# A hand-written MLP order on one Trainium2 core: the passage from one unit to the next, rewritten

## The chip, the core and the metric

The kernel runs on one core of a Trainium2 chip. TensorE (PE in the profile) multiplies matrices into PSUM, which has eight banks of 128 partitions x 512 fp32 numbers. ScalarE (ACT) and VectorE (DVE) empty these banks and prepare operands in SBUF. SyncE (SP) issues the loads of weights, GpSimd (POOL) the DMAs that add results into the residual stream. Each engine works through its own instructions in the order in which the program has them, and waits on semaphores for what others must deliver. The metric is the device time of one execution in microseconds, the median of several.

## The reference, cut to what matters

A trunk of two layers over 256 tokens of width 2048, in fp32, with another attention in each layer. The change touches the MLP's order above all, and the projections' slightly:

```python
for i in range(DEPTH):                       # 2
    proj = _rmsnorm(x, g_attn[i]) @ w_in[i]  # 2048 x 5120
    ...
    x = x + merged @ w_out[i]                # 2048 x 2048
    hm = _rmsnorm(x, g_mlp[i])
    x = x + jnp.square(jax.nn.relu(hm @ w_mlp1[i])) @ w_mlp2[i]   # 2048 x 8192, 8192 x 2048
return _rmsnorm(x, g_final)
```

## The kernel before

**Products.** An fp32 operand is split into a rounded high part and the rest: ACT copies it to the high part (L117), DVE subtracts that from it (L118). A product is then three matmuls into the same bank, high by high, high by low and low by high (`passes`, L609 to L611).

**The MLP.** The 8192 hidden features are taken in eight units of 1024. Unit 0 is multiplied plainly (`up_plain`), in the part that a scheduler orders. Units 1 to 7 use a 2x2 block scheme with seven products, p1 to p7, in place of eight. A unit's products take eight steps over the 2048 inner features; a step adds 21 matmuls of 512 columns, three for each product, into seven banks. The eighth bank rotates: it takes the down product's groups (`psd`) and the turned blocks (`pu`).

**Factors.** The weights of a step are combined first (`up_weights`, `prep_up`). From two loaded tiles b and o DVE makes the sums s (L229) and o (L233, L235), and each of b, one half of o, s and the new o is split into a high and a low part: bh and bl, oh, sh and sl, th and tl. These are 6.95 us of DVE and some 3.4 us of ACT per step. p1 and p3 use b, p2 uses oh, p5 and p7 use s, p6 and p4 use t. Seven buffers hold one step's factors.

**The hand-written order** (`tc.manual_schedule()`, L736 to L763). While unit c+1 is multiplied up, unit c is multiplied down. Eight groups g make a unit: in group g the kernel issues one step of the next unit (`step_up`), the factors of the step after (`prep_up`), and 24 matmuls of the down product (`group_down`), whose bank ACT copies to `part` with a scale (L703) and POOL adds to x by DMA (L704). The down product's weights come in pieces of 256 rows, `raw_d`, split into `hi_d` and `lo_d` (`prep_down`); four buffers of each hold one bank's.

**The passage.** With g = 6 a unit's products end. `end_up` empties the seven banks with DVE additions (L659 to L668) into four blocks u0 to u3; ACT applies relu and square to each (L614, L615). With g = 7 the first step of the unit after follows into the banks as they come free. With g = 0 comes the second step, and between its products PE turns the four blocks: four transposes each into the rotating bank (`pu`, L681), which ACT and DVE split into `hT` (L117, L118). The next block, or the next `psd`, can start when DVE has read the bank. There are six passages in each layer, twelve in all; the start of the written order, with unit 0's blocks, and its end, with unit 7's, are like half a passage each. In names such as `pu_012` the digits are the layer, the unit and the block; `psd0031` is layer 0, unit 0, column block 3, token half 1.

Of the kernel before, what the change touches and what calls it, by code (L numbers as in the profile page):

```python
# [9 lines left out]
F32 = mybir.dt.float32  # L10
# [28 lines left out]
WH = 4  # L39
# [19 lines left out]
def trunk(ctx: ExitStack, tc: tile.TileContext, x, mem, g_attn, w_in, w_out, lambda_qk,  # L59
# [69 lines left out]
    def gemm_feat(w, acts, nm, raws=(None,) * 4):  # L129

        ps = [bank([P, 2, 256], f"ps_{nm}_{j}", True) for j in range(2)]
        for pc in range(4):
            wt = weights(w[pc * 512:(pc + 1) * 512, :], 4, 256, f"{nm}_{pc}", raws[pc])
            for kk in range(4):
                k = 4 * pc + kk
                hi, lo = wt[kk]
                a = acts[k // 4][:, k % 4]
                for j in range(2):
                    last = k == KT - 1
                    cols = slice(j * P, (j + 1) * P)  # L140

                    def low(**f):
                        nc.tensor.matmul(ps[j][:, 0, :], lo[:, cols], a[:, 0, :], **f)  # L143

                    def high(**f):
                        nc.tensor.matmul(ps[j].rearrange("p h t -> p (h t)"), hi[:, cols], a.rearrange("p h t -> p (h t)"), **f)  # L146

                    if last:
                        low(start=False, stop=False)
                        high(start=False, stop=True)  # L150
                    else:
                        high(start=(k == 0), stop=False)
                        low(start=False, stop=False)
# [56 lines left out]
    def up_weights(w, kp, f0, nm):  # L210
# [25 lines left out]
        t1, t3 = pieces(s, 2, "s")  # L236
        t2, t4 = pieces(o, 2, "t")
# [203 lines left out]
    for i in range(DEPTH):  # L441
# [175 lines left out]
        def up_plain():  # L617

            u = {}
            for f in range(2):  # L620
                ps = [bank([P, 512], f"pu0_{i}{f}{t}", True) for t in range(2)]
                for kp in range(KP):
                    wt = weights(w_mlp1[i][kp * 256:(kp + 1) * 256, f * 512:(f + 1) * 512], 2, 512, f"u0{i}{f}{kp}")
                    for a in range(2):
                        for t in range(2):
                            passes(ps[t], comb[kp][:, 2 * t + a], *wt[a], kp == a == 0, kp == KP - 1 and a == 1)
                for t in range(2):
# [6 lines left out]
        def prep_up(c, kp):  # L634

            making = up_weights(w_mlp1[i], kp, c * 1024, f"{i}{c}{kp}")
            for _ in range(2):
# [4 lines left out]
        def step_up(c, kp, turns=None, prep=None):  # L642
# [3 lines left out]
            for n, (hi, lo) in facts.pop((c, kp)).items():  # L646
                if turns and n in ("p1", "p3", "p5", "p6"):
                    next(turns)
                    if n in ("p1", "p5"):
                        next(prep)  # L650
                passes(banks[c][n], comb[kp][:, FACTORS.index(n)], hi, lo, kp == 0, kp == KP - 1)

        def end_up(c):

# [13 lines left out]
            nc.vector.tensor_tensor(c21, u3, ps["p4"], op=ALU.add)  # L668
            yield
            squared(m22, m22, -1.0)  # L670
            squared(c21, c21, 1.0)
            ublk[c] = ((c11, 0, 0), (m12, 0, 1), (c21, 1, 0), (m22, 1, 1))
# [12 lines left out]

        def prep_down(c, n, halves):

            for h in halves:
                for k in (4 * h, 4 * h + 2):
                    r0 = c * 1024 + k * P  # L690
# [144 lines left out]
```

## Time and profile before

| | us |
|---|---|
| time, median of 3 runs | 2298.21 |
| lowest and highest | 2297.55, 2300.5 |
| profiled execution | 2299.35 |
| its span, first to last instruction | 2297.6 |
| PE busy | 2207.4 |
| DVE busy | 1715.9 |
| ACT busy | 1332.0 |
| granted PE clock, mean share of full | 0.981 |

The span is what the trace covers; 1.75 us of the profiled execution lie around it. A busy engine isn't one at its peak: PE's matmuls are pipelined, so that each is listed with 0.39 us while the next starts 0.23 us later, and the durations of ACT and DVE overlap in the same way by some 0.1 us. What counts is the distance from one start to the next.

### The profile page before, as it was taken

The page shows a single profiled execution, that of the slowest core. Times are in us where ns is not written, and L with a number is a line of the kernel's source. Part 1 is how long each engine was busy: PE and PEld are TensorE (multiplying, and loading weights), DVE is VectorE, ACT ScalarE, POOL GpSimd, SP SyncE. Part 2 cuts the span into 40 slices and gives each one's busy share as a digit, 9 for nine tenths or more (in the row PEclk, how much of TensorE's full clock was granted, in tenths as well). Part 3 has the DMA queues.
Part 4 walks back from the last instruction along what each step waited for, and adds up shares of the span by engine and source line. Part 5 has one row for each costly group of instructions (what it writes and reads, how often), then busy time and mean ns, then how long its engine had stood idle before and what let it go on. Part 6 is the DMA issues. An engine that isn't in the chain of part 4 may idle for free.

```text
span 2297.6 us, 28469 instructions
## 1 busy us (share of the span) xinstructions
PE 2207.4 (96%) x10358; PEld 1814.3 (79%) x10358; DVE 1715.9 (75%) x2084; ACT 1332.0 (58%) x1840; POOL 115.4 (5%) x146
## 2 busy tenths in 40 slices
PE   9999999999999999999999999999999999999998
PEld 7888878887787787777878888887877778777786
DVE  6557766758888888888866665665888888888875
ACT  7445554655666666666655554465666666666664
POOL 0000000000000000000000000000000000000000
PEclk9999999999999999999999999999999999999999
DMA  7664555666676676676745556566767668667664
GB/s 242 193 192 151 169 163 187 184 181 212 187 235 188 197 225 196 206 218 182 212 135 185 164 169 183 194 188 178 220 184 233 191 186 238 196 195 230 186 205 142
DMA packets 262399, 443.50 MB, mean 193 GB/s; under 512 B 14497, under 2 KB 80242, under 8 KB 262002
## 3 DMA queue, kind: packets, MB, share of 16 engines
q1 hardware_dynamic: 245856, 412.14, 57.0%
q0 software_dynamic: 16128, 29.37, 7.2%
q8 instruction: 81, 1.33, 0.2%
q14 instruction: 60, 0.49, 0.1%
q10 hardware_dynamic: 274, 0.17, 0.0%
HBM read 409.12 MB, written 3.15 MB: 179 GB/s over the span
## 4 chain that ended last, share of the span: by engine, by line
PE 83%; DVE 8%; ACT 6%; issue 3%; DMA 0%; ACTq 0%; DVEq 0%; SPq 0%; POOL 0%; POOLq 0%
PE psd L609 8%; PE psd L611 8%; PE psd L610 8%; PE p L609 6%; PE p L610 6%; PE p L611 6%; PE ps_q L146 4%; PE ps_k L146 4%; PE pso L166 2%; PE pso L167 2%; PE pso L165 2%; PE ps_k L143 2%; PE ps_q L143 2%; PE psv L166 2%; PE psv L167 2%
## 5 line engine op out<-in xcount | busy, mean ns | idle before, releaser
L609 PE MATMUL psd<-hi_d,hT 128*128 128x512 f32 x1008 | 395.2, 393 | 3.8 <-ACT hT L117 3.3
L611 PE MATMUL psd<-hi_d,hT 128*128 128x512 f32 x1008 | 393.6, 391 | 2.9 <-DVE hT L118 2.9
L610 PE MATMUL psd<-lo_d,hT 128*128 128x512 f32 x1008 | 393.5, 391 | 0.0
L118 DVE TENSOR_TENSOR lo_d<-raw_d,hi_d 128x1024 fp32r<-128x1024 f32 x252 | 298.0, 1222 | 104.3 <-ACT hi_d L117 104.3
L117 ACT ACTIVATE hi_d<-raw_d 128x1024 fp32r<-128x1024 f32 x252 | 256.9, 1051 | 14.2 <-PE psd L611 5.8
L609 PEld LDWEIGHTS psd<-hi_d,hT 128*128 128x128 f32 x1008 | 190.0, 189 | 50.0 <-DVE hT L118 6.6
L117 ACT ACTIVATE th<-o 128x1024 fp32r<-128x1024 f32 x112 | 119.0, 1062 | 185.3 <-DVE o L235 184.6
L611 PEld LDWEIGHTS psd<-hi_d,hT 128*128 128x128 f32 x1008 | 190.2, 189 | 43.1 <-DVE hT L118 3.6
L610 PEld LDWEIGHTS psd<-lo_d,hT 128*128 128x128 f32 x1008 | 190.1, 189 | 39.1
L118 DVE TENSOR_TENSOR bl<-b,bh 128x1024 fp32r<-128x1024 f32 x112 | 136.9, 1223 | 70.0 <-ACT bh L117 70.0
L704 POOL DMA_DIRECT2D x_sb<-part x112 | 97.3, 869 | 1271.9 <-ACT part L703 1271.9
L117 ACT ACTIVATE sh<-s 128x1024 fp32r<-128x1024 f32 x112 | 118.7, 1059 | 63.0 <-DVE s L229 44.0
L118 DVE TENSOR_TENSOR tl<-o,th 128x1024 fp32r<-128x1024 f32 x112 | 137.2, 1225 | 5.8
L229 DVE TENSOR_TENSOR s<-b,o 128x1024 f32<-128x1024 f32 x112 | 136.4, 1218 | 4.7 <-DMA o<-in_w_mlp_dram 4.7
L146 PE MATMUL ps_q<-xT,hi_q 128*128 128x512 f32 x384 | 138.4, 401 | 0.0
L146 PE MATMUL ps_k<-xT,hi_k 128*128 128x512 f32 x384 | 138.0, 399 | 0.0
L118 DVE TENSOR_TENSOR sl<-s,sh 128x1024 fp32r<-128x1024 f32 x112 | 136.4, 1218 | 0.0
L703 ACT ACTIVATE part<-psd,rsq 128x512 f32<-128x512 f32 x112 | 76.8, 686 | 99.5 <-PE psd L611 97.6
L117 ACT ACTIVATE bh<-b 128x1024 fp32r<-128x1024 f32 x112 | 118.1, 1054 | 19.2 <-PE p L610 18.6
L609 PE MATMUL p<-bh,cb_xm 128*128 128x512 f32 x224 | 96.7, 432 | 12.7 <-DVE t L661 12.7
L143 PE MATMUL ps_q<-xT,lo_q 128*128 128x256 f32 x384 | 107.1, 284 | 0.0
L143 PE MATMUL ps_k<-xT,lo_k 128*128 128x256 f32 x384 | 106.7, 283 | 0.0
(331 smaller groups left out, 4993.9 us busy)
## 6 DMA issues: line engine op xcount, KB each, us to landing
raw_d<-in_w_mlp_dram SPq DMA_DIRECT2D x252, 512.0 KB, 5.8
b<-in_w_mlp_dram SPq DMA_DIRECT2D x112, 512.0 KB, 4.4
o<-in_w_mlp_dram SPq DMA_DIRECT2D x112, 512.0 KB, 3.8
x_sb<-part POOLq DMA_DIRECT2D x112, 256.0 KB, 5.6
raw_q<-in_w_in_dram SPq DMA_DIRECT2D x48, 512.0 KB, 3.7
raw_k<-in_w_in_dram SPq DMA_DIRECT2D x48, 512.0 KB, 3.7
raw_v<-in_w_in_dram SPq DMA_DIRECT2D x48, 512.0 KB, 3.7
raw_o<-in_w_out_dram SPq DMA_DIRECT2D x48, 512.0 KB, 3.8
```

What stands on the lines that cost most here:

```text
L117: nc.scalar.activation(dst_hi, src, AF.Copy)
L118: nc.vector.tensor_tensor(dst_lo, src, dst_hi.bitcast(F32), op=ALU.subtract)
L143: nc.tensor.matmul(ps[j][:, 0, :], lo[:, cols], a[:, 0, :], **f)
L146: nc.tensor.matmul(ps[j].rearrange("p h t -> p (h t)"), hi[:, cols], a.rearrange("p h t -> p (h t)"), **f)
L166: nc.tensor.matmul(ps[t], ah, lo, start=False, stop=False)
L167: nc.tensor.matmul(ps[t], al, hi, start=False, stop=last and kk == 3)
L229: nc.vector.tensor_tensor(s, b, o[:, 0:1].to_broadcast([P, 2, 512]), op=ALU.add)
L609: nc.tensor.matmul(ps, acts[:, 0, :], hi, start=first, stop=False)
L610: nc.tensor.matmul(ps, acts[:, 0, :], lo, start=False, stop=False)
L611: nc.tensor.matmul(ps, acts[:, 1, :], hi, start=False, stop=last)
L703: nc.scalar.activation(part, ps, AF.Copy, scale=rsq[:, t:t + 1])
L704: nc.gpsimd.dma_start(x_sb[:, t, n * 512:(n + 1) * 512], part, accum_op=ALU.add)
```

## The change

No instruction is added or taken away in the MLP; they are issued in another order.

- The first step of a unit multiplies in the order p1, p2, p6, p3, p7, p5, p4 (before: p1, p3, p2, p5, p7, p6, p4, as all other steps).
- Behind the last step of a unit, ACT makes bh, oh, sh of the next factors ahead of the relu and square of the last two blocks, and `hi_d` of the next bank's first piece ahead of th.
- `prep_down` is cut into a high and a low part. On DVE the next bank's first `lo_d` stays ahead of the first turned block, the second goes behind it.
- Of the four turned blocks, three lie in the second step, behind p1, p2 and p7, and the fourth in the third step, behind two of its products.
- The factors of unit 1's first two steps are written ahead of the end of the plain part.
- `gemm_feat` issues the high products of both output halves, then the low ones.

```diff
@@ gemm_feat: for j in range(2) moves into low() and high()
-                for j in range(2):
...
-                        high(start=(k == 0), stop=False)
-                        low(start=False, stop=False)
+                def low(**f):
+                    for j in range(2):
+                        nc.tensor.matmul(ps[j][:, 0, :], lo[:, j * P:(j + 1) * P], a[:, 0, :], **f)
...
+                    high(start=(k == 0), stop=False)
+                    low(start=False, stop=False)
@@ step_up
-        def step_up(c, kp, turns=None, prep=None):
+        def step_up(c, kp, between=None):
...
-            for n, (hi, lo) in facts.pop((c, kp)).items():
-                if turns and n in ("p1", "p3", "p5", "p6"):
-                    next(turns)
-                    if n in ("p1", "p5"):
-                        next(prep)
+            order = ("p1", "p2", "p6", "p3", "p7", "p5", "p4") if kp == 0 else ("p1", "p3", "p2", "p5", "p7", "p6", "p4")
+            made = facts.pop((c, kp))
+            for j, n in enumerate(order):
+                if between and j in between:
+                    between[j]()
+                hi, lo = made[n]
                 passes(banks[c][n], comb[kp][:, FACTORS.index(n)], hi, lo, kp == 0, kp == KP - 1)
@@ end_up
             yield
+            squared(c21, c21, 1.0)
             squared(m22, m22, -1.0)
-            squared(c21, c21, 1.0)
@@ prep_down
-                    dw[c, n, k], dw[c, n, k + 1] = weights(w, 2, 512, nm, load_weights(w, 2, 512, nm, k == 6))
+                    piece_hi(c, n, k)
+                    piece_lo(c, n, k)
@@ the written order
-        up_plain()
+        first = up_plain()
+        next(first)
         with tc.manual_schedule():
             run(prep_up(1, 0))
+            run(first)
+            prep = prep_up(1, 1)
+            next(prep)
             step_up(1, 0)
-            run(prep_up(1, 1))
-            prep_down(0, 0, (0,))
+            run(prep)
+            piece_hi(0, 0, 0)
+            piece_hi(0, 0, 2)
+            piece_lo(0, 0, 0)
...
                     if g == 0:
-                        step_up(uc, kp, to_hT(c), prep)
-                        prep_down(c, 0, (1,))
-                    elif uc < NC:
-                        step_up(uc, kp)
-                    ending = end_up(c + 1) if g == 6 else iter(())
-                    next(ending, None)
-                    run(prep)
-                    next(ending, None)
...
+                        turned = to_hT(c)
+
+                        def turn_first():
+                            next(turned)
+                            piece_lo(c, 0, 2)
+                            next(prep)
+
+                        def turn_second():
+                            next(turned)
+                            next(prep)
+
+                        step_up(uc, kp, {1: turn_first, 3: turn_second, 5: lambda: next(turned)})
+                        prep_down(c, 0, (1,))
+                        run(prep)
+                    elif g == 1:
+                        step_up(uc, kp, {2: lambda: run(turned)})
+                        run(prep)
+                    elif g == 6:
+                        step_up(uc, kp)
+                        ending = end_up(c + 1)
+                        next(ending)
+                        run(prep)
+                        next(ending)
+                    elif g == 7:
+                        if uc < NC:
+                            step_up(uc, kp)
+                        for _ in range(3):
+                            next(prep, None)
+                        run(ending)
+                        piece_hi(*more, 0)
+                        run(prep)
+                        piece_hi(*more, 2)
+                        piece_lo(*more, 0)
+                    else:
+                        step_up(uc, kp)
+                        run(prep)
...
```

In the program, ACT's order in the first passage of the first layer, from the copy `part` of the last but one down group to that of the last, was this (u2 and u3 are unit 1's last two blocks, `_021` the factors of unit 2's second step, d0100 and d0102 the first two pieces of unit 1's down weights):

```order
L703 ACTIVATE part0030_5272<-psd0030_5247,rsq0_4242 128x512
L614 ACTIVATE u3_01_5235<-u3_01_5235 128x512
L615 ACTIVATE u3_01_5235<-u3_01_5235 128x512
L614 ACTIVATE u2_01_5234<-u2_01_5234 128x512
L615 ACTIVATE u2_01_5234<-u2_01_5234 128x512
L117 ACTIVATE bh_021_5314<-b_021_5307 128x1024
L117 ACTIVATE oh_021_5312<-o_021_5309 128x512
L117 ACTIVATE sh_021_5322<-s_021_5311 128x1024
L117 ACTIVATE th_021_5326<-o_021_5309 128x1024
L117 ACTIVATE hi_d0100_5332<-raw_d0100_5330 128x1024
L117 ACTIVATE hi_d0102_5338<-raw_d0102_5336 128x1024
L703 ACTIVATE part0031_5367<-psd0031_5342,rsq0_4242 128x512
```

The same piece of ACT's order after the change (the functions are the same, some at other lines):

```order
L723 ACTIVATE part0030_5272<-psd0030_5247,rsq0_4242 128x512
L117 ACTIVATE bh_021_5310<-b_021_5303 128x1024
L117 ACTIVATE oh_021_5308<-o_021_5305 128x512
L117 ACTIVATE sh_021_5318<-s_021_5307 128x1024
L615 ACTIVATE u2_01_5234<-u2_01_5234 128x512
L616 ACTIVATE u2_01_5234<-u2_01_5234 128x512
L615 ACTIVATE u3_01_5235<-u3_01_5235 128x512
L616 ACTIVATE u3_01_5235<-u3_01_5235 128x512
L698 ACTIVATE hi_d0100_5328<-raw_d0100_5326 128x1024
L117 ACTIVATE th_021_5330<-o_021_5305 128x1024
L698 ACTIVATE hi_d0102_5336<-raw_d0102_5334 128x1024
L723 ACTIVATE part0031_5365<-psd0031_5340,rsq0_4242 128x512
```

The two squares moved behind bh, oh and sh, and `hi_d0100` ahead of `th`; the second `part` stays last.

DVE's order in the same passage, from the end of the second step's factors through the turned blocks (`pu`), was:

```order
L118 TENSOR_TENSOR tl_021_5327<-o_021_5309,th_021_5326 128x1024
L118 TENSOR_TENSOR lo_d0100_5333<-raw_d0100_5330,hi_d0100_5332 128x1024
L118 TENSOR_TENSOR lo_d0102_5339<-raw_d0102_5336,hi_d0102_5338 128x1024
L118 TENSOR_TENSOR hT010_5370<-pu_010_5372,hT010_5370 128x4x128
L229 TENSOR_TENSOR s_022_5383<-b_022_5379,o_022_5381 128x1024
L118 TENSOR_TENSOR hT011_5371<-pu_011_5389,hT011_5371 128x4x128
L118 TENSOR_TENSOR hT010_5370<-pu_012_5402,hT010_5370 128x4x128
L118 TENSOR_TENSOR bl_022_5410<-b_022_5379,bh_022_5409 128x1024
L118 TENSOR_TENSOR hT011_5371<-pu_013_5419,hT011_5371 128x4x128
```

DVE's order there after the change:

```order
L118 TENSOR_TENSOR tl_021_5331<-o_021_5305,th_021_5330 128x1024
L704 TENSOR_TENSOR lo_d0100_5338<-raw_d0100_5326,hi_d0100_5328 128x1024
L118 TENSOR_TENSOR hT010_5371<-pu_010_5373,hT010_5371 128x4x128
L704 TENSOR_TENSOR lo_d0102_5380<-raw_d0102_5334,hi_d0102_5336 128x1024
L229 TENSOR_TENSOR s_022_5386<-b_022_5382,o_022_5384 128x1024
L118 TENSOR_TENSOR hT011_5372<-pu_011_5395,hT011_5372 128x4x128
L118 TENSOR_TENSOR bl_022_5403<-b_022_5382,bh_022_5402 128x1024
L118 TENSOR_TENSOR hT010_5371<-pu_012_5412,hT010_5371 128x4x128
```

The second `lo_d` moved from ahead of the first block to behind it, bl ahead of the third, and the fourth block (`pu_013`) out of this piece: it stands behind tl_022, eight places on.

PE's order there, from the last matmul of unit 0's down product into the second step of unit 2, was:

```order
L611 MATMUL psd0031_5342<-hi_d0036_5179,hT001_4638 128x512
L681 MATMUL pu_010_5372<-ident_91,u0_01_5232 128x128 x4
L609 MATMUL p1_02_5279<-bh_021_5314,cb_xm01_3663 128x512
L610 MATMUL p1_02_5279<-bl_021_5315,cb_xm01_3663 128x512
L611 MATMUL p1_02_5279<-bh_021_5314,cb_xm01_3663 128x512
L681 MATMUL pu_011_5389<-ident_91,u1_01_5233 128x128 x4
L609 MATMUL p3_02_5280<-bh_021_5314,cb_xm01_3663 128x512
L610 MATMUL p3_02_5280<-bl_021_5315,cb_xm01_3663 128x512
L611 MATMUL p3_02_5280<-bh_021_5314,cb_xm01_3663 128x512
L609 MATMUL p2_02_5281<-oh_021_5312,cb_xm01_3663 128x512
L610 MATMUL p2_02_5281<-oh_021_5312,cb_xm01_3663 128x512
L611 MATMUL p2_02_5281<-oh_021_5312,cb_xm01_3663 128x512
```

PE's order there after the change:

```order
L612 MATMUL psd0031_5340<-hi_d0036_5179,hT001_4639 128x512
L610 MATMUL p1_02_5275<-bh_021_5310,cb_xm01_3663 128x512
L611 MATMUL p1_02_5275<-bl_021_5311,cb_xm01_3663 128x512
L612 MATMUL p1_02_5275<-bh_021_5310,cb_xm01_3663 128x512
L687 MATMUL pu_010_5373<-ident_91,u0_01_5232 128x128 x4
L610 MATMUL p3_02_5276<-bh_021_5310,cb_xm01_3663 128x512
L611 MATMUL p3_02_5276<-bl_021_5311,cb_xm01_3663 128x512
L612 MATMUL p3_02_5276<-bh_021_5310,cb_xm01_3663 128x512
L610 MATMUL p2_02_5277<-oh_021_5308,cb_xm01_3663 128x512
L611 MATMUL p2_02_5277<-oh_021_5308,cb_xm01_3663 128x512
L612 MATMUL p2_02_5277<-oh_021_5308,cb_xm01_3663 128x512
L687 MATMUL pu_011_5395<-ident_91,u1_01_5233 128x128 x4
```

Three matmuls of p1 stand ahead of the first block, and six, of p3 and p2, between the first and the second, where there were three.

## Rows read from the trace of the kernel before

**Rows 1.** The page's first part: busy time, share of the span and instructions of each engine.

```profile
PE 2207.4 (96%) x10358; PEld 1814.3 (79%) x10358; DVE 1715.9 (75%) x2084; ACT 1332.0 (58%) x1840; POOL 115.4 (5%) x146
```

**Rows 2.** The table of waits: engine, line and tile, what it waited for; us in total, times, the longest.

```profile
PE pu L681 <- ACT part L703: 34.7, 12, 2.9
...
PE pu L681 <- DVE hT L118: 13.7, 8, 5.2
...
PE p L609 <- DVE t L661: 12.7, 12, 1.1
```

**Rows 3.** Busy time by stretches of the trace: the first, the eighth, the eleventh and the last of the twelve passages, and their sum. Columns: start and end, length, busy us (instructions) of PE, PEld (its weight loads), DVE, ACT, POOL; granted PE clock, DMA share, GB/s.

```profile
596.02:625.89 29.87, 25.20 (x107) 18.94 (x106) 24.36 (x29) 19.04 (x26) 1.73 (x2) 0.94 0.52 151
...
1774.95:1806.02 31.07, 26.45 (x107) 19.91 (x106) 24.36 (x29) 19.05 (x26) 1.74 (x2) 0.89 0.50 146
...
2051.64:2080.87 29.23, 24.00 (x108) 17.88 (x106) 24.37 (x29) 19.06 (x26) 1.75 (x2) 1.00 0.53 154
2142.07:2172.04 29.97, 25.17 (x107) 18.90 (x106) 24.36 (x29) 19.05 (x26) 1.73 (x2) 0.94 0.52 147
sum 366.79, PE 308.72 PEld 232.40 DVE 292.46 ACT 228.62 POOL 20.82; mean PE 25.73 PEld 19.37 DVE 24.37 ACT 19.05 POOL 1.74
```

**Rows 4.** The same view, of the rest of a unit behind the third passage, of the first part of that passage, and of the stretch behind its longest wait.

```profile
809.25:870.45 61.20, 61.20 (x271) 50.68 (x270) 53.92 (x56) 38.31 (x44) 5.18 (x6) 1.00 0.81 236
778.67:782.70 4.03, 2.50 (x10) 1.45 (x9) 3.92 (x7) 1.94 (x4) 0.00 (x0) 1.00 0.77 264
796.11:799.47 3.36, 3.36 (x11) 2.68 (x12) 1.77 (x2) 0.60 (x1) 0.00 (x0) 0.53 0.87 245
```

**Rows 5.** The timeline of PE in the third passage of the first layer: start, us, engine, line, operation, out<-in, count, and in brackets the idle time before it with its releaser.

```profile
778.67 0.39 PE L609 MATMUL p<-bh,cb_xm 128*128 128x512 f32 x1
...
780.57 0.50 PE L609 MATMUL p<-bh,cb_xm 128*128 128x512 f32 x1 [1.06 <-DVE t L661]
...
782.70 0.47 PE L609 MATMUL p<-sh,cb_xm 128*128 128x512 f32 x1 [0.48 <-ACT u L614]
...
785.56 0.39 PE L609 MATMUL psd<-hi_d,hT 128*128 128x512 f32 x1
...
790.78 0.39 PE L611 MATMUL psd<-hi_d,hT 128*128 128x512 f32 x1
794.04 0.66 PE L681 MATMUL pu<-ident,u 128*128 128x128 f32 x4 [2.88 <-ACT part L703]
...
796.11 0.99 PE L681 MATMUL pu<-ident,u 128*128 128x128 f32 x4 [0.72 <-DVE hT L118]
...
803.68 0.50 PE L609 MATMUL psd<-hi_d,hT 128*128 128x512 f32 x1
...
809.25 0.39 PE L609 MATMUL p<-bh,cb_xm 128*128 128x512 f32 x1
```

**Rows 6.** The timeline of ACT there.

```profile
783.19 0.67 ACT L703 ACTIVATE part<-psd,rsq 128x512 f32<-128x512 f32 x1
783.76 0.62 ACT L614 ACTIVATE u<-u 128x512 f32<-128x512 f32 x1
...
786.14 1.04 ACT L117 ACTIVATE bh<-b 128x1024 fp32r<-128x1024 f32 x1
787.09 0.62 ACT L117 ACTIVATE oh<-o 128x512 fp32r<-128x512 f32 x1
787.61 1.04 ACT L117 ACTIVATE sh<-s 128x1024 fp32r<-128x1024 f32 x1
790.46 1.06 ACT L117 ACTIVATE th<-o 128x1024 fp32r<-128x1024 f32 x1 [1.81 <-DVE o L235]
791.43 1.99 ACT L117 ACTIVATE hi_d<-raw_d 128x1024 fp32r<-128x1024 f32 x2
793.32 0.67 ACT L703 ACTIVATE part<-psd,rsq 128x512 f32<-128x512 f32 x1
```

**Rows 7.** The timeline of DVE there.

```profile
779.23 0.68 DVE L660 TENSOR_TENSOR u<-t,p 128x512 f32<-128x512 f32 x1
...
781.27 0.69 DVE L664 TENSOR_TENSOR u<-t,p 128x512 f32<-128x512 f32 x1
...
783.19 0.68 DVE L668 TENSOR_TENSOR u<-t,p 128x512 f32<-128x512 f32 x1
...
787.21 1.22 DVE L118 TENSOR_TENSOR bl<-b,bh 128x1024 fp32r<-128x1024 f32 x1 [2.21 <-ACT bh L117]
...
791.55 1.22 DVE L118 TENSOR_TENSOR tl<-o,th 128x1024 fp32r<-128x1024 f32 x1
792.70 2.35 DVE L118 TENSOR_TENSOR lo_d<-raw_d,hi_d 128x1024 fp32r<-128x1024 f32 x2
795.36 0.69 DVE L118 TENSOR_TENSOR hT<-pu,hT 128x512 fp32r<-128x512 f32 x1 [0.32 <-ACT hT L117]
```

**Rows 8.** The start of the written order in the first layer: PE's second turned block, and the stretch around it in the view of rows 3.

```profile
520.85 1.11 PE L681 MATMUL pu<-ident,u 128*128 128x128 f32 x4 [5.18 <-DVE hT L118]
...
510.06:534.82 24.76, 19.56 (x82) 15.57 (x80) 18.11 (x20) 14.69 (x20) 0.00 (x0) 0.86 0.39 121
```

**Rows 9.** The page's costliest groups: the high (512 columns) and low (256 columns) matmuls of the key projections. Columns: count, busy us, mean ns of one, idle before.

```profile
L146 PE MATMUL ps_k<-xT,hi_k 128*128 128x512 f32 x384 | 138.0, 399 | 0.0
L143 PE MATMUL ps_k<-xT,lo_k 128*128 128x256 f32 x384 | 106.7, 283 | 0.0
```

More of the change, by code (lines that the diff above doesn't have):

```diff
@@ L137, in gemm_feat, with high @@
                 a = acts[k // 4][:, k % 4]
-                for j in range(2):
[L139 to L148, printed above, removed]
-                        low(start=False, stop=False)
-                        high(start=False, stop=True)
-                    else:
-                        high(start=(k == 0), stop=False)
-                        low(start=False, stop=False)
+                def low(**f):
+                    for j in range(2):
+                        nc.tensor.matmul(ps[j][:, 0, :], lo[:, j * P:(j + 1) * P], a[:, 0, :], **f)
+                def high(**f):
+                    for j in range(2):
+                        nc.tensor.matmul(ps[j].rearrange("p h t -> p (h t)"), hi[:, j * P:(j + 1) * P],
+                                         a.rearrange("p h t -> p (h t)"), **f)
+                if k == KT - 1:
+                    low(start=False, stop=False)
+                    high(start=False, stop=True)
+                else:
+                    high(start=(k == 0), stop=False)
+                    low(start=False, stop=False)
         return ps
@@ L636, in prep_up @@
             making = up_weights(w_mlp1[i], kp, c * 1024, f"{i}{c}{kp}")
-            for _ in range(2):
+            for _ in range(3):
                 next(making)
@@ L755, in trunk @@
                     more = (c, n + 1) if n < 3 else (c + 1, 0)
-                    if t == 1:
+                    if g == 0:
+                        turned = to_hT(c)
[21 more added lines that the diff above has]
+                            step_up(uc, kp)
+                        for _ in range(3):
+                            next(prep, None)
[4 more added lines that the diff above has]
+                        piece_lo(*more, 0)
+                    else:
+                        step_up(uc, kp)
+                        run(prep)
@@ L757, in trunk @@
+                    if t == 1 and g < 7:
                         prep_down(*more, (0,))
                     add_down(c, n, t, group_down(c, n, t, False))
-                    run(ending)
-                    if t == 1 and n < 3:
+                    if t == 1 and g < 7:
                         prep_down(*more, (1,))
+            piece_lo(NC - 1, 0, 2)
             prep_down(NC - 1, 0, (1,))
```

21 lines of the change are left out of this document (17 added, 4 removed).

## The prediction

> **What bounds the kernel now.** I read the page first: TensorE (PE) is busy for 96% of the span [rows 1], so time can come only from PE's gaps, its clock, or less work for it. The change takes no matmul away. The table of waits then says where PE stands still: three lines, some 61 us together, two of them twelve times each [rows 2]. Twelve is two layers times six passages from one unit's products to the next one's. I therefore cut the MLP into stretches: a passage runs from the first matmul of a new unit's first step to the first matmul of its third step. The twelve add up to 366.79 us, 30.57 in the mean, the first 29.87 and the last 29.97; DVE is busy for 24.37 of them, ACT for 19.05 [rows 3]. The rest of a unit, 61.20 us, has PE busy for all of it, with DVE at 53.92 [rows 4]. So between passages there is nothing to gain, and a slower DVE there would have 7.28 us of room. In a passage PE issues 90 matmuls of 512 columns, one every 0.227 us (from 785.56 to 790.78 are 23 steps [rows 5]), and sixteen short transposes (four are listed with 0.66 us and take some 0.4 by the next start): some 22.1 us of work. About 8.4 us of each passage is waiting or half clock: 101 us in the twelve.
>
> The order of one passage, the third of the first layer, shows where they lie [rows 5]: 1.06 us at 780.57 for a bank that DVE must empty, 0.48 at 782.70, 2.88 at 794.04 for the copy `part` on ACT, 0.72 at 796.11. After the long wait the granted clock falls: it is 0.53 from 796.11 to 799.47, nearly the lower of its two levels (1.2 and 2.4 GHz), against 1.00 from 778.67 to 782.70, where the two shorter waits leave PE busy for 2.50 of 4.03 us [rows 4].
>
> **The change part by part.** I replay this passage with the new order by hand, each engine taking its own queue in turn, with durations from its rows. Starts follow each other more closely than the listed durations say: ACT 0.95 for 1024 columns, 0.52 for a copy of 512, 1.19 for one relu with its square, 0.57 for `part`; DVE 1.15 and 0.60 [rows 6, 7].
>
> *The first step's products.* PE needs old p2's bank after p1 (free when DVE ends at 779.91), then p6's, then p3's (free at 781.96) [rows 7]. In the new order p1 p2 p6 p3 p7 p5 p4 it waits 0.6 us ahead of p2 and 0.6 ahead of p3, and nothing behind them: p3 starts at 782.02, p7 at 782.8, p5 783.5, p4 784.2, and the down group `psd` at 784.85, not 785.56. Minus 0.7 us. The bank of p4 is free when `part` ends at 783.86 [rows 6], the last unit block u2 is read at 783.87 [rows 7]: both just in time, so I give this term an uncertainty of 0.5 either way.
>
> *The activations later.* After `part` at 783.19 ACT ran two pairs of relu and square (2.38 us) ahead of bh, oh, sh; now these three come first, and `hi_d` of the next bank stands ahead of `th`. `th` waited 1.81 us for DVE's o, whose chain started with bl at 787.21, behind bh [rows 6, 7]. Now bh starts at 783.76, bl about 784.9, o is ready at 788.0. ACT runs without a gap: bh 783.76, oh 784.71, sh 785.23, the four squares from 786.18, `hi_d` 788.56, `th` 789.51, second `hi_d` 790.47, and `part` 791.43, not 793.32. It ends at 792.10 and the first turned block `pu` starts at 792.15. The delayed squares are read only by the third and fourth block, so their delay costs nothing; the other `hi_d` buffers free up with the previous group, which is early enough. PE reaches the block after `psd` and the three matmuls of p1 now put ahead of it, at about 791.05. Its wait is 1.1 us in place of 2.88.
>
> *The bank copied at once, and the turned blocks over two steps.* DVE now has one `lo_d` (1.15) ahead of the first block's hT, not two. tl ends at about 791.8, `lo_d` at 792.95, hT runs 793.47 to 794.16, and the second block starts at 794.21; PE, with six matmuls of p3 and p2 between, has waited 0.2. The other `lo_d` and the next factor's s stand on DVE ahead of the second hT: 2.3 us, so hT runs at 796.36 and the third block starts at 797.10, with a wait of 1.0 behind six matmuls. bl and the third hT end at 799.11 and `psd` starts at 799.16 after 0.2 more. Before it started at 803.68 [rows 5]. It takes 5.54, so the third step begins at 804.7, 26.03 us after 778.67. The fourth block goes into that step with its four transposes, +0.5: 26.53 in comparison with 30.58. This block waits for the next `part`, done about 0.4 us before PE comes to it, and its hT, on DVE behind two `lo_d`, the o chain, sl and tl, is made at about 807.6, while the second `psd` reads it with its thirteenth matmul, at 804.7 + 0.5 + 33 × 0.227 = 812.7: hidden, with 5 us to spare. SP and POOL keep their orders, the weight loads of these steps are issued as before, and they landed well ahead; I cost them at nothing.
>
> All twelve passages should now be alike, for they differ mostly by clock: 366.79 − 12 × 26.53 = 48.4 us. The replay of each wait is uncertain by some 0.8 us a passage, hence ±10 us.
>
> *The clock.* I count it at full speed, since waits of 1.2 us at most are of the size of those in 778.67 to 782.70, where it stayed 1.00 [rows 4]. The one passage that kept 1.00 throughout took 29.23 [rows 3], so falls cost 30.57 − 29.23 = 1.34 in the mean, and this goes too; it is within the 48.4. The Trainium skill speaks against me here: in "TensorE: Matmul & The Clock Gate", section "A second HAM failure mode: psum-queue depth-cycling", it says in substance that a kernel which cycles through PSUM banks with small waits between its groups can make the clock swing between its two levels. By that rule four small waits would be no better than the long one; the two in 778.67 to 782.70 do not agree with it, and no row shows four in a row. It makes a rival below.
>
> *The two starts of the written order* (once a layer). At 520.85 the second turned block waits 5.18 us for hT on DVE, in a stretch of 24.76 us at clock 0.86 [rows 8]. Six matmuls now stand in that wait, and DVE has one `lo_d` less ahead: 1.5 us each, 3 for both; bounds 0, if it only waits elsewhere, and 6, if the clock stays up too. Factors made ahead of the plain part's end: the scheduler of the front part already had them there, so 0, with −2 to +2 as bounds.
>
> *The projections.* `gemm_feat` swaps two neighbours: hi, hi, lo, lo for two halves. Its 512 and 256 column matmuls occur 384 times each for keys, with 399 and 283 ns [rows 9], and for queries as often; the same instructions run back to back, so 0, bounds ±2 us. At the end of each layer only two squares change places: 0.
>
> Sum: 48.4 + 3 = 51.4. The profiled execution took 2299.35 us, its span 2297.6 and 1.75 around it, so 2248.0; the median of the runs shown is 1.14 lower, which gives 2246.9: 2247 us, own range 2238 to 2258 (±10 of the replay).
>
> **The rivals.**
> *The clock still falls in every passage.* For it: all the passages but one have a clock under 1.00 now [rows 3], and the waits before the second and third block, 1.1, 0.2, 1.0, 0.2, lie within 8 us. Against: [rows 4]. Then a passage gains 29.23 − 26.53 = 2.7 us, or 0.5 less if each fall is like the dearest (some 31.07 − 29.23 = 1.84 instead of 1.34): 27 to 32 for twelve, and 1 for the starts: about 2267 us, 2262 to 2272. This is also what the skill's rule above would give.
>
> *The waits get shorter than in my replay.* Engines may slip past each other earlier than starts in the old rows tell, and the second `lo_d` may fit in DVE's gaps. My replay has 1.2 us of waits in the first step and 2.5 later; all of it gone would be another 44 us, 2203; half of it 2225. For it: DVE is not busy for 6.2 us of a passage [rows 3]. Against: each wait rests on a chain of two engines.
>
> *Slower: the fourth block comes late.* Its hT is queued on ACT behind `th` and on DVE behind tl of the next factors, and the next `psd` reads it. If DVE, with 24.37 us of work in a passage of 26.53, falls behind, PE waits at that `psd` one for one. It decides from 9 us of lateness: 5 of cover plus the 4.04 gained. At 11 us, 2 us lost per passage, it is 2298 + 24 = 2322. Against: in the middle of a unit DVE has 7.28 us of room [rows 4].
>
> *No change.* The waits go, but DVE sets the pace of the passage, which then keeps its 30.57: 2298. Against: DVE's work per unit is 24.37 + 53.92 = 78.3 of 30.58 + 61.20 = 91.8 us, of 87.7 after.
>
> **How the numbers follow.** Forecast 0.66, clock falls 0.14, shorter waits 0.12, no change 0.04, slower 0.04. The range 2228 to 2272 leaves out some half of the shorter waits and the last two, 0.14 in all. About 0.2% of the time, 4.6 us, is what a measurement of this kernel can tell from none: faster 0.92, same 0.04, slower 0.04.
>
> **What would show it.** In the changed kernel's trace, passages of 26 to 27 us; on PE two waits of about 0.6 in the new unit's first step, 1.1 ahead of the first turned block behind ACT `part`, 1.0 ahead of the third behind DVE's hT; no long wait and a granted clock near 1.00 in them, and the middle of a unit still without a gap. The forecast is wrong if the passage keeps a wait of over 2 us, if the clock is 0.9 there, or if a new wait appears at the second `psd` of a unit.

## The result and the profile after

| | before | changed |
|---|---|---|
| time, median of 4 runs, us | 2299.36 | 2243.48 |
| profiled execution, us | 2299.35 | 2243.37 |
| its span, us | 2297.6 | 2241.6 |
| granted PE clock, mean | 0.981 | 0.995 |

The ratio is 0.9758, 95% interval 0.9741 to 0.9775: 55.9 us faster, where 51 had been forecast. Times are medians, and one execution among all those below, of the kernel called `v3_chain`, took 7553.77 us and is left out of its median. The page's busy time and PE's lines in the table of waits of the changed kernel:

```profile
PE 2181.0 (97%) x10358; PEld 1794.2 (80%) x10358; DVE 1711.9 (76%) x2084; ACT 1326.3 (59%) x1840; POOL 115.7 (5%) x146
```

```profile
PE pu L687 <- DVE hT L118: 16.7, 14, 3.4
...
PE pu L687 <- ACT part L723: 11.3, 12, 1.0
...
PE p L610 <- DVE u L666: 6.6, 12, 0.6
```

PE lost 26.4 us of busy time with the same number of matmuls, for the greater part clock. The wait for `part` went from 34.7 us, 2.9 each, to 11.3, 1.0 each; in the first step 12.7, 1.1 each, became 6.6, 0.6 each, and the second wait there, 0.48 before, is 0.32 (below); the wait for hT grew from 13.7 to 16.7 and occurs 14 times, not 8 [rows 2]. The stretches of the passages, first, eighth, last and the sum of twelve, and the third step behind the third passage:

```profile
592.98:619.02 26.04, 23.31 (x103) 17.60 (x102) 23.49 (x28) 18.34 (x25) 1.74 (x2) 1.00 0.59 172
...
1740.24:1766.29 26.05, 23.32 (x104) 17.60 (x103) 23.50 (x28) 18.35 (x25) 1.74 (x2) 1.00 0.60 177
...
2091.09:2117.12 26.03, 23.39 (x103) 17.59 (x102) 23.48 (x28) 18.35 (x25) 1.73 (x2) 1.00 0.59 176
sum 312.44, PE 280.15 PEld 211.14 DVE 281.87 ACT 219.85 POOL 20.87; mean PE 23.35 PEld 17.60 DVE 23.49 ACT 18.32 POOL 1.74
...
794.46:805.15 10.69, 10.69 (x50) 8.84 (x49) 9.25 (x11) 6.86 (x9) 0.86 (x1) 1.00 0.71 200
```

All are alike, at clock 1.00. The sum is 54.35 below [rows 3]; the fourth block made the third step 10.69 us, where a step and its group took 10.20 before:

```profile
809.25:819.45 10.20, 10.20 (x46) 8.45 (x45) 10.05 (x11) 6.47 (x8) 0.86 (x1) 1.00 0.79 227
```

That is 0.49 x 12 = 5.9 back: the passages gave 48.5 us. The third passage's timeline on PE, in comparison with [rows 5]:

```profile
769.81 0.47 PE L610 MATMUL p<-oh,cb_xm 128*128 128x512 f32 x1 [0.55 <-DVE u L666]
...
771.76 0.51 PE L610 MATMUL p<-bh,cb_xm 128*128 128x512 f32 x1 [0.32 <-DVE u L670]
...
774.63 0.39 PE L610 MATMUL psd<-hi_d,hT 128*128 128x512 f32 x1
...
781.88 0.66 PE L687 MATMUL pu<-ident,u 128*128 128x128 f32 x4 [0.97 <-ACT part L723]
...
783.95 0.66 PE L687 MATMUL pu<-ident,u 128*128 128x128 f32 x4
...
786.82 0.66 PE L687 MATMUL pu<-ident,u 128*128 128x128 f32 x4 [0.83 <-DVE hT L118]
...
788.89 0.50 PE L610 MATMUL psd<-hi_d,hT 128*128 128x512 f32 x1
```

It starts at 768.42, so the blocks come 13.46, 15.53 and 18.40 us into it and the down group at 20.47. On ACT and DVE, in comparison with [rows 6, 7]:

```profile
773.52 1.05 ACT L117 ACTIVATE bh<-b 128x1024 fp32r<-128x1024 f32 x1
...
781.16 0.67 ACT L723 ACTIVATE part<-psd,rsq 128x512 f32<-128x512 f32 x1
```

```profile
781.48 1.22 DVE L704 TENSOR_TENSOR lo_d<-raw_d,hi_d 128x1024 fp32r<-128x1024 f32 x1
783.20 0.69 DVE L118 TENSOR_TENSOR hT<-pu,hT 128x512 fp32r<-128x512 f32 x1 [0.51 <-ACT hT L117]
783.81 1.22 DVE L704 TENSOR_TENSOR lo_d<-raw_d,hi_d 128x1024 fp32r<-128x1024 f32 x1
784.94 1.22 DVE L229 TENSOR_TENSOR s<-b,o 128x1024 f32<-128x1024 f32 x1
786.08 0.68 DVE L118 TENSOR_TENSOR hT<-pu,hT 128x512 fp32r<-128x512 f32 x1
```

ACT's `part` starts 12.74 us into the passage, 14.65 before. DVE waits 0.51 ahead of the first hT, so its one `lo_d` there had room; the second hT comes right behind the other `lo_d` and s.

The rest of the gain lies outside the passages. The two starts and the last stretch, first of the changed kernel, then of before:

```profile
498.15:592.98 94.83, 91.44 (x399) 75.41 (x398) 73.12 (x76) 54.55 (x64) 5.40 (x6) 0.96 0.70 214
1558.54:1652.53 93.99, 90.58 (x400) 74.34 (x399) 73.12 (x76) 54.56 (x64) 5.28 (x6) 0.98 0.71 216
2184.26:2241.60 57.34, 46.51 (x233) 38.85 (x231) 33.87 (x50) 24.63 (x40) 2.16 (x3) 0.95 0.44 143
```

```profile
499.18:596.02 96.84, 91.64 (x400) 75.27 (x398) 73.26 (x76) 54.46 (x64) 5.38 (x6) 0.96 0.69 211
1587.33:1683.17 95.84, 90.59 (x400) 74.17 (x398) 73.21 (x76) 54.47 (x64) 5.27 (x6) 0.98 0.69 211
2238.69:2297.60 58.91, 48.07 (x233) 40.01 (x231) 33.86 (x50) 24.63 (x40) 2.15 (x3) 0.92 0.43 139
```

The starts gave 2.01 + 1.85 = 3.9 us. The end gave 1.6, at clock 0.95 in place of 0.92 with the same work. What remains of the span's 56.0 is 2.1 us of the front parts.

### The profile page after: what moved, and what is told of

It is laid out like the page before. It is cut to its first block, busy times and chain, and to the rows that moved or that the text cites. A ratio compares the mean times of both kernels' runs of the same rounds, so it can differ in the third digit from the quotient of the medians.

```text
span 2241.6 us, 28416 instructions
## 1 busy us (share of the span) xinstructions
PE 2181.0 (97%) x10358; PEld 1794.2 (80%) x10358; DVE 1711.9 (76%) x2084; ACT 1326.3 (59%) x1840; POOL 115.7 (5%) x146
## 4 chain that ended last, share of the span: by engine, by line
PE 81%; ACT 7%; DVE 7%; issue 3%; DMA 1%; ACTq 0%; DVEq 0%; SPq 0%; POOL 0%; POOLq 0%
PE psd L610 8%; PE psd L612 8%; PE psd L611 8%; PE p L610 6%; PE p L611 5%; PE p L612 5%; PE ps_k L145 4%; PE ps_q L145 4%; PE pso L166 2%; PE pso L167 2%; PE pso L165 2%; PE ps_q L141 2%; PE ps_k L141 2%; PE psv L165 2%; PE psv L166 2%
## 5 line engine op out<-in xcount | busy, mean ns | idle before, releaser
L118 DVE TENSOR_TENSOR tl<-o,th 128x1024 fp32r<-128x1024 f32 x112 | 137.3, 1226 | 22.1 <-ACT th L117 16.7
L145 PE MATMUL ps_k<-xT,hi_k 128*128 128x512 f32 x384 | 122.3, 398 | 0.0
L145 PE MATMUL ps_q<-xT,hi_q 128*128 128x512 f32 x384 | 122.0, 399 | 0.0
L118 DVE TENSOR_TENSOR lo_v<-raw_v,hi_v 128x1024 fp32r<-128x1024 f32 x48 | 58.8, 1225 | 50.2 <-ACT hi_v L117 50.1
L610 PE MATMUL p<-bh,cb_xm 128*128 128x512 f32 x224 | 89.7, 400 | 3.9 <-DVE u L670 3.9
L610 PE MATMUL p<-sh,cb_xm 128*128 128x512 f32 x224 | 89.8, 401 | 0.0
```

What stands on the lines that cost most here:

```text
L118: nc.vector.tensor_tensor(dst_lo, src, dst_hi.bitcast(F32), op=ALU.subtract)
L610: nc.tensor.matmul(ps, acts[:, 0, :], hi, start=first, stop=False)
```

## The experiments

The leading theory: one serial chain sets the passage, ACT's queue up to `part`, then turned block, hT on ACT, hT on DVE, block by block; an edit counts only as far as it shortens that chain. Rival one: each edit is worth the term the prediction gave it. Rival two: only the falls of the clock count. A third, that DVE's load sets the pace, came in with the later runs. Times below have the changed kernel's 2243.48 to compare with; stretches are read from the profiles, each of one execution, and starts count from the passage's start. Words in code style at the heads are the names that the expectations use.

**The first step's order undone** (`u1_order`).

```diff
-            order = ("p1", "p2", "p6", "p3", "p7", "p5", "p4") if kp == 0 else ("p1", "p3", "p2", "p5", "p7", "p6", "p4")
+            order = ("p1", "p3", "p2", "p5", "p7", "p6", "p4")
```

> The changed kernel with the first step's products in the old order p1 p3 p2 p5 p7 p6 p4. Theory (one serial chain sets the passage: ACT's queue up to `part`, then turned block, hT on ACT, hT on DVE, three times): the down group starts 0.7 us later, but ACT reaches `part` only 0.9 us after that group has ended, so the wait ahead of the first turned block shrinks by what the first step loses; 0 to 0.1 us a passage, 2243 to 2245 us. Rival one (each edit is worth the term that the prediction gave it): 0.7 us a passage, 12 x 0.7 = 8 us, 2252. Rival two (only falls of the clock count): no fall, 2243.

2244.09 us (ratio to before 0.9759, 0.9744 to 0.9774). PE in the passage that starts at 769.96:

```profile
776.82 0.39 PE L610 MATMUL psd<-hi_d,hT 128*128 128x512 f32 x1
...
783.41 0.66 PE L687 MATMUL pu<-ident,u 128*128 128x128 f32 x4 [0.31 <-ACT part L723]
```

The group starts 0.65 later, the wait shrinks from 0.97 to 0.31, and the block starts at 13.45 as before: this edit is worth nothing beside the others. Rival one falls here. With the chain freed, below, no wait for `part` is left ahead of the first block, so there the 0.65 should count; no run undoes the order there.

**Four blocks in one step** (`u2_blocks`).

```diff
-                        step_up(uc, kp, {1: turn_first, 3: turn_second, 5: lambda: next(turned)})
+                        step_up(uc, kp, {1: turn_first, 3: turn_second, 5: lambda: next(turned), 6: lambda: run(turned)})
...
-                        step_up(uc, kp, {2: lambda: run(turned)})
+                        step_up(uc, kp)
```

> The changed kernel with all four turned blocks in the second step, the fourth ahead of the last product. Theory: the fourth block adds one round of the chain, 2.06 us from block to block, ahead of the second step's down group, and takes 0.49 off the third step: +1.57 us a passage, 19 us, 2262. The wait it makes ahead of that group is about 0.9 us, no fall of the clock. Rival one: the same. Rival two (only falls count): 2243.

2269.77 us (0.9869, 0.9854 to 0.9884). Fourth block and down group in the passage that starts at 777.15:

```profile
797.62 0.66 PE L687 MATMUL pu<-ident,u 128*128 128x128 f32 x4 [0.72 <-DVE hT L118]
...
799.69 0.50 PE L610 MATMUL psd<-hi_d,hT 128*128 128x512 f32 x1 [0.72 <-DVE hT L118]
```

The group starts at 22.54, and the two steps end 1.60 us later in every passage, as the chain says, without one fall of the clock: 19.2 us. Rival two falls. The other 7 us of the time lie outside the passages: 2.1 in the two starts, which have four blocks in one step too, and 5.0 ahead of the first layer's written order, where this execution's clock fell twice (0.91 from 20 to 40 and from 380 to 400 us, in both 1.00 in the changed kernel); why it fell there is open.

**ACT's old order** (`u3_acts`).

```diff
                     elif g == 7:
...
-                        for _ in range(3):
-                            next(prep, None)
-                        run(ending)
+                        run(prep)
                         piece_hi(*more, 0)
-                        run(prep)
                         piece_hi(*more, 2)
...
                     add_down(c, n, t, group_down(c, n, t, False))
+                    if g == 6:
+                        run(ending)
```

> The changed kernel with ACT's old order: the last two blocks' relu and square right behind the first `part`, and the first `hi_d` behind `th`. Theory: the second `part` ends 1.9 us later and with it the whole chain: the wait ahead of the first turned block is 0.97 + 1.9 = 2.9 us again, 12 x 1.9 = 23 us; and since the old wait of that length came with a fall of the clock in eleven of twelve passages, falls come back, about 1.34 us each, 16 us: 2282 us, or 2266 without falls. Rival two (only falls count): the part without falls is 0, 2259.

2275.34 us (0.9893, 0.9878 to 0.9908). Two passages, and PE's first block in each:

```profile
864.68:892.80 28.12, 23.30 (x104) 17.60 (x103) 23.57 (x28) 18.56 (x25) 1.74 (x2) 1.00 0.57 162
...
1850.08:1879.71 29.63, 25.67 (x104) 19.96 (x102) 23.74 (x28) 18.55 (x25) 1.73 (x2) 0.88 0.52 152
```

```profile
880.21 0.66 PE L687 MATMUL pu<-ident,u 128*128 128x128 f32 x4 [3.05 <-ACT part L723]
...
1865.61 1.11 PE L687 MATMUL pu<-ident,u 128*128 128x128 f32 x4 [3.05 <-ACT part L723]
```

The wait is 3.00 to 3.05 us in all twelve, and the block starts at 15.53, 2.08 later: 25 us. The same wait brought the clock down in eight passages and left it at 1.00 in four. The twelve are 343.01 us, 30.6 more than in the changed kernel, so the eight falls cost 5.6 in all, less than expected: 0.3 to 0.55 in the six passages at a clock of 0.94, 1.4 and 1.5 in the two at 0.88. In the four without a fall PE waits 0.83 for hT ahead of the third block, in the eight with one it doesn't: the slow stretch lay in part where PE would have waited.

**Both `lo_d` ahead of the first block** (`u4_bank`).

```diff
...
                             next(turned)
-                            piece_lo(c, 0, 2)
                             next(prep)
...
                         piece_hi(*more, 2)
                         piece_lo(*more, 0)
+                        piece_lo(*more, 2)
...
```

> The changed kernel with both `lo_d` of the next bank ahead of the first turned block's hT on DVE, as before. Theory: the first hT comes 0.6 us later, but nothing but s then stands ahead of the second hT, which comes 0.2 us earlier; the third block starts at the same time or 0.2 us earlier: 0 to -0.2 us a passage, 2241 to 2244 us: this edit brought nothing. Rival one (each edit its term): 0.6 us or more a passage lost, 2250 or more.

2243.21 us (0.9752, 0.9736 to 0.9768). The down group in the passage that starts at 771.05:

```profile
791.27 0.50 PE L610 MATMUL psd<-hi_d,hT 128*128 128x512 f32 x1
```

The group starts at 20.22, 0.24 us earlier in every passage than in the changed kernel: moving the second `lo_d` behind the first block costs 2.9 us there, in place of bringing any. At the two starts the same move brings 1.5. What is left of the difference, some 1.4 us, doesn't show in the time: the four executions of this kernel lie between 2241.77 and 2246.37. The profiled one, at 2246.37, loses more by the clock ahead of the first layer's written order and at the end.

**The front undone** (`u5_front`): `gemm_feat` interleaved as before, unit 1's factors behind the plain part and behind the first step.

```diff
@@ gemm_feat: for j in range(2) around low() and high() again
...
-        first = up_plain()
-        next(first)
+        run(up_plain())
...
-            run(first)
-            prep = prep_up(1, 1)
-            next(prep)
             step_up(1, 0)
-            run(prep)
+            run(prep_up(1, 1))
```

> The changed kernel with the projections' two halves interleaved as before and the factors of unit 1 written behind the plain part's end and behind the first step as before. Theory: both are worth nothing; the two starts gained by the turned blocks and the `lo_d`, which stay: 2243 us, from 2241 to 2247 by where the front part's clock falls lie. Rival one (each edit its term, bounds of the prediction): the projections up to 2 us, the factors up to 2 us: 2247.

2246.46 us (0.9771, 0.9757 to 0.9784). Layer 1 from the first memory scores to the MLP's written order, here, in the changed kernel and before:

```profile
1205.63:1561.48 355.85, 355.85 (x1847) 302.86 (x1846) 218.18 (x298) 187.46 (x295) 0.70 (x1) 1.00 0.59 176
```

```profile
1203.37:1558.54 355.17, 355.17 (x1848) 302.46 (x1846) 217.43 (x298) 186.79 (x295) 0.70 (x1) 1.00 0.59 177
```

```profile
1231.47:1587.33 355.86, 355.86 (x1848) 302.87 (x1846) 218.17 (x298) 187.61 (x296) 0.70 (x1) 1.00 0.59 177
```

PE has no gap in any of them, and the projections' new order takes 0.7 us off. In layer 0 the like stretch took 369.31 us before and 368.81 in the changed kernel, 0.5 less, 0.1 of it in PE's gaps; here it can't be compared, for the clock fell in it once (0.91 from 380 to 400 us), which makes up most of the 3.0 us by which this kernel's time is longer. Placing the factors early shortened nothing: the starts are 93.80 and 93.87 us here, not longer than 94.83 and 93.99. It is also less than the list of the change says: in the diff the first step's factors stand ahead of the plain part's end, but of the second step's only s, and that behind it, ahead of the first step's products.

**ACT's order alone** (`a1_acts`), on the kernel before: with both `lo_d` ahead of the first block.

```diff
...
+                    if g == 7:
+                        for _ in range(3):
+                            next(prep, None)
+                        run(ending)
+                        piece_hi(*more, 0)
+                        run(prep)
+                        piece_hi(*more, 2)
+                        piece_lo(*more, 0)
+                        piece_lo(*more, 2)
+                    else:
+                        run(prep)
...
-                    run(ending)
```

> The kernel before with ACT's new order alone (relu and square of the last two blocks behind bh, oh, sh, and the first `hi_d` ahead of `th`); both `lo_d` ahead of the first block, four blocks in one step, the products in the old order. Theory: `part` ends 1.9 us earlier, the wait ahead of the first block is 1.1 us, the down group starts 2.8 us earlier than in the third passage before, and the clock doesn't fall: a passage of 27.8 us in place of 30.57 in the mean, 33 us for twelve, 2266. Rival one (each edit its term): 1.8 us a passage and the falls, 38 us, 2262. Rival two (only falls count): 1.34 us a passage, 16 us, 2283.

2269.40 us (0.9870, 0.9856 to 0.9884). Two passages, and the second block in each:

```profile
685.34:713.24 27.90, 24.05 (x108) 17.88 (x106) 24.24 (x29) 18.98 (x26) 1.73 (x2) 1.00 0.56 164
...
2113.76:2142.97 29.21, 25.43 (x108) 19.17 (x107) 24.20 (x29) 18.67 (x26) 1.73 (x2) 0.94 0.52 153
```

```profile
701.40 0.66 PE L682 MATMUL pu<-ident,u 128*128 128x128 f32 x4 [1.26 <-DVE hT L118]
...
2129.82 1.12 PE L682 MATMUL pu<-ident,u 128*128 128x128 f32 x4 [1.26 <-DVE hT L118]
```

Nine passages take 27.85 to 27.90 us, where the theory has 27.8; in three the clock fell, behind two waits close together, 0.93 to 0.98 ahead of the first block and 1.26 ahead of the second. The same two waits stand in the other nine, at clock 1.00. The twelve are 338.44: this edit alone brings 28.4 of the passages' 48.5 us, some 16 of them by the shorter passages at clock 1.00 (27.88 for 29.23), the rest by falls that are gone.

**s behind the second hT** (`v1_sums`). Would the third block's wait go, and would it stay gone?

```diff
                         def turn_first():
                             next(turned)
                             piece_lo(c, 0, 2)
-                            next(prep)
...
-                        step_up(uc, kp, {1: turn_first, 3: turn_second, 5: lambda: next(turned)})
+                        step_up(uc, kp, {1: turn_first, 3: turn_second, 5: turn_second})
```

> The changed kernel with s of the next factors behind the second turned block's hT on DVE instead of ahead of it, and bl behind the third. Theory (serial chain): the 0.83 us wait ahead of the third block goes, blocks follow each other by 2.07 us, the second step's down group starts at 19.66 instead of 20.46 us behind the passage's start: 12 x 0.80 = 10 us, 2234. Rival two (only falls of the clock count): 2243. Rival three (DVE's load sets the pace: what it does later, PE waits for later): 2243, with a new wait in the third step.

2242.34 us (0.9752, 0.9738 to 0.9767): the group does start at 19.66, but the third step, 11.2 us, gives back 0.5 of the 0.8. Its rows on ACT and PE:

```profile
794.42 1.06 ACT L117 ACTIVATE th<-o 128x1024 fp32r<-128x1024 f32 x1 [2.19 <-DVE o L235]
795.39 0.67 ACT L723 ACTIVATE part<-psd,rsq 128x512 f32<-128x512 f32 x1
```

```profile
796.11 0.66 PE L687 MATMUL pu<-ident,u 128*128 128x128 f32 x4 [0.31 <-ACT part L723]
```

The fourth block waits for `part`, `part` stands behind `th`, and `th` waits for DVE's o. The bound moved one step on, to the same queue. The time and the new wait are also those of rival three; the last two runs tell the two apart.

**The chain freed** (`v3_chain`, and `v3_again`, the same kernel once more). `part` ahead of the second `hi_d`, each `lo_d` behind one hT, s behind the third.

```diff
                         run(prep)
-                        piece_hi(*more, 2)
-                        piece_lo(*more, 0)
...
                         def turn_first():
                             next(turned)
-                            piece_lo(c, 0, 2)
-                            next(prep)
+                            piece_hi(c, 0, 2)
+                            piece_lo(c, 0, 0)
...
                         def turn_second():
                             next(turned)
+                            piece_lo(c, 0, 2)
+
+                        def turn_third():
+                            next(turned)
                             next(prep)
 
-                        step_up(uc, kp, {1: turn_first, 3: turn_second, 5: lambda: next(turned)})
+                        step_up(uc, kp, {1: turn_first, 3: turn_second, 5: turn_third})
...
```

> The changed kernel with the chain freed: `part` ahead of the second `hi_d` on ACT, each `lo_d` behind one turned block's hT on DVE, s behind the third. Theory: `part` ends 0.9 us earlier, the first block starts at 12.6 instead of 13.45 us, three blocks at 2.07 us from each other, the down group at 18.8 instead of 20.46: 1.69 us a passage, 20 us for twelve and about 1 for each start: 2222 us. Rival three (DVE's load sets the pace): s, bl and the later `lo_d` come too late for the down group's ninth product or for the third step, and half or more of it is given back: 2233 or more.

> v3_chain once more for its stretches. Theory: the second step's down group at 18.8 us behind the passage's start, and a wait of about 1 us for `part` in the third step, behind th. Rival three: that group itself late or slow, at its ninth product behind `lo_d`.

2243.87 us (0.9755, 0.9740 to 0.9770), not the 2222 expected, and 2241.05 in the second run, whose profile is read here. The down group starts at 18.8 us as expected, and the third step is 1.3 us longer than in the changed kernel, nearly all of it in front of the fourth block. ACT's `th` ahead of `part`, and the block on PE:

```profile
792.87 1.06 ACT L117 ACTIVATE th<-o 128x1024 fp32r<-128x1024 f32 x1 [2.98 <-DVE o L235]
...
794.55 0.66 PE L687 MATMUL pu<-ident,u 128*128 128x128 f32 x4 [1.10 <-ACT part L723]
```

**`part` ahead of `th`**, added to `v1_sums` (`v5_part_first`) and to `v3_chain` (`v4_chain_part`). The lines for the former; the latter has `range(2)`:

```diff
                         prep_down(c, 0, (1,))
-                        run(prep)
+                        for _ in range(1):
+                            next(prep)
...
                     add_down(c, n, t, group_down(c, n, t, False))
+                    if g == 0:
+                        run(prep)
```

> v1_sums with one more move: in the second step's group ACT makes `part` ahead of th of the next factors, and DVE's tl follows later. Theory (what v1_sums gave back is ACT's queue: its third step has a wait of 0.31 us for `part`, which stood behind th, and th behind DVE's o): the wait goes, th and tl are 0.7 us later and still 1 us ahead of their product, so the 0.80 us of v1_sums is kept, nearly: 0.74 us a passage against the changed kernel, 9 us, and about 1 for the starts: 2233 us, or 2235 if the front part's clock falls once as in v1_sums. Rival three (DVE's load sets the pace): 2241, the loss moves to tl's product.

> v3_chain with the same move. Theory: v3_chain's gain was given back in the third step too, where its th is later than in v1_sums by two `lo_d`; with `part` ahead of th the first down group's 1.69 us a passage stays, less up to 0.6 for the later `lo_d`: 1.1 to 1.7 us, 13 to 20 us, 2222 to 2231 us. Rival three: DVE, which now makes s, two `lo_d`, bl, o, oh, sl and tl behind the third block, is late for the third step: 2240 or more.

2236.53 us (0.9716, 0.9703 to 0.9730) and 2226.94 us (0.9675, 0.9662 to 0.9688). In both the third step is back at 10.67 us. The faster one's first, third and last passage; the four blocks of the third, of which none waits; and ACT between its third and fourth block, where `part` now waits for PE alone:

```profile
592.90:617.29 24.39, 23.34 (x103) 17.59 (x102) 21.61 (x26) 17.43 (x24) 1.73 (x2) 1.00 0.62 176
765.04:789.43 24.39, 23.32 (x104) 17.61 (x103) 21.61 (x26) 17.45 (x24) 1.75 (x2) 1.00 0.60 170
2073.73:2098.10 24.37, 23.29 (x103) 17.59 (x102) 21.61 (x26) 17.42 (x24) 1.73 (x2) 1.00 0.61 176
```

```profile
777.64 0.66 PE L687 MATMUL pu<-ident,u 128*128 128x128 f32 x4
779.71 0.66 PE L687 MATMUL pu<-ident,u 128*128 128x128 f32 x4
781.78 0.66 PE L687 MATMUL pu<-ident,u 128*128 128x128 f32 x4
...
790.79 0.60 PE L687 MATMUL pu<-ident,u 128*128 128x128 f32 x4
```

```profile
789.62 0.69 ACT L723 ACTIVATE part<-psd,rsq 128x512 f32<-128x512 f32 x1 [2.24 <-PE psd L612]
790.30 1.06 ACT L117 ACTIVATE th<-o 128x1024 fp32r<-128x1024 f32 x1
```

This is 16.5 us less than the changed kernel's time; by the ratios, each to the kernel before as run beside it (0.9675 and 0.9758), it is 19. Rival three falls: DVE does the same work as before and nothing waits for it in the third step; what `v1_sums` and `v3_chain` lost was the place of `part` in ACT's queue.

## Why the prediction was right

- *The passages.* Forecast 26.53 us each, with the fourth block's half microsecond; measured 26.04 + 0.49. The sum 48.4 was 48.5. The replay's starts held within 0.1 us: first block 13.48 forecast, 13.46 measured, third 18.43 and 18.40, group 20.49 and 20.47. Its single waits held less well (the second in the first step 0.6 forecast, 0.32 measured; 0.2 ahead of the second block and of the group, where PE didn't wait): the starts are what the sum rests on.
- *The first step's products*, "minus 0.7 us": the group did start 0.7 us earlier, yet undoing it cost nothing. The step is right as a start, and as a gain it would be wrong: PE then waits for ACT, whose `part` doesn't move for it. The replay's sum has it so, for its first block starts when `part` ends.
- *The activations later.* 1.9 us of the chain were forecast; with the old order back it is 2.08, and 28.4 of 48.5 us come with this edit alone, the falls that it ends included.
- *The bank copied at once.* Told as part of the gain, it costs 0.24 us a passage and brings 1.5 us in the two starts: taking a `lo_d` from ahead of the first hT put it, with s, ahead of the second.
- *The turned blocks over two steps.* The replay did not give it a price of its own; undone, it is 1.60 us a passage and 2.1 us in the two starts.
- *The clock.* No fall in the twelve passages, as forecast, by rows that held two waits close together. The Trainium skill's rule in "TensorE: Matmul & The Clock Gate", section "A second HAM failure mode: psum-queue depth-cycling", did not show in the changed kernel, at waits of 0.55, 0.32, 0.97 and 0.83. In the kernel with ACT's order alone, waits of 0.93 to 0.98 and 1.26 came with a fall in three passages of twelve, so waits of about the size that the forecast took for harmless are not always so: its step was right for this order, with less margin than the text gave it, and the rival's chance of 0.14 was not too high.
- *The shortfall of 4.6 us*, 51.4 forecast against 56.0 of the spans: the starts 3.9 for 3, the projections some 1.2 for 0 (0.7 and 0.5, inside their bounds of 2), the end 1.6 for 0, the passages 0.1, and some 0.8 at the beginning and at the end of layer 0, whose cause stays open. That all of these went the same way was not foreseen.
- *The end's 1.6* is clock alone (0.95 for 0.92); in two of the experiments, `u4_bank` and `v5_part_first`, this stretch was 1.5 us longer again at 0.92, in the latter without an edit near it. So it can't be counted as the change's: it goes with where an execution's falls lie.

## What to carry to other kernels

When one engine waits for a copy, replay the queue of the engine that makes the copy, and move everything behind it that is not read sooner. Price each edit within the replay and not by itself: an earlier start upstream is worth nothing while another queue sets the next one. When a wait is gone, look one step on in the same queue: here the next block's `part` stood behind the same kind of work, and both moves together were worth 16.5 us, where the first alone was worth next to nothing.

## What was not expected of the hardware

The same wait of 3.00 to 3.05 us at the same place left the clock at 1.00 in four passages of one execution and was followed by a fall in eight. Waits of about 1 us, two in a row, were followed by one in three passages of twelve. A wait's length alone therefore does not settle whether the clock falls. What a fall cost varied too: at a passage's clock of 0.94 it was 0.3 to 0.55 us where a wait of 0.83 went with it, and 1.2 to 1.3 with ACT's order alone, where no such wait followed; at 0.88 it was 1.4 to 1.5. Pairing the projections' matmuls by length, two of 512 columns and then two of 256, took 0.7 us off 355.9 us in which PE had no gap.
